# A hybrid decoder layer on one core: row sums of w_ada in PSUM, left factors and weight sums made by VectorE, later keys, other banks

## The chip, the cores and the metric

The kernel runs on one core of one Trainium2 chip. A core has five engines that run their own instruction queues and wait for each other by semaphores: TensorE (PE, matrix products, whose results go to PSUM), VectorE (DVE), ScalarE (ACT), GpSimd (POOL) and SyncE (SP, which here issues every large transfer). [...] The metric is the device time of one execution in microseconds; lower is better.

## The reference

One layer for a sequence of 1024 tokens and a model width of 2048, all in fp32:

```python
mod = silu(c) @ w_ada + b_ada                  # c: (1, 2048), w_ada: (2048, 6144)
shift, scale, gate = split(mod, 3)
h = rms_norm(x, norm_gain) * (1 + scale) + shift
q_sb, k_sb, v_sb, z_sb, q_r, k_r, v_r, z_r = split(h @ w_in)     # w_in: (2048, 8192), 8 parts of 1024
oa = stick_breaking_attention(rms_norm(q_sb), rms_norm(k_sb), v_sb) * silu(z_sb)   # 8 heads of 128
ob = group_norm(chunkwise_retention(rotary(q_r), rotary(k_r), v_r)) * silu(z_r)    # 8 heads of 128
x = x + gate * (concat(oa, ob) @ w_out)        # w_out: (2048, 2048)
```

Stick-breaking attention: `A[t,s] = beta[t,s] * prod_{s<j<t} (1 - beta[t,j])` for s < t, with beta the sigmoid of the scaled scores. Retention: chunks of 128 tokens with a decaying state between them.

## The kernel before

**The products with w_in and w_out** are made with Strassen's scheme on 2 x 2 blocks: seven products P1 to P7 for each pair of 128-column blocks of the weights (a *group*), and sums of blocks on both sides. Each operand is split into a high part in float32r and a low part (the rest), and a product is made of three matmuls of 128 x 128 by 512 columns (high x high, high x low, low x high; `mm3`, L150 to L152). A group's product is a *step* of four such triples. After each triple the program calls `tick()`.

There are 80 groups: *a* (16, tile names e: the first half of the contraction, for attention's columns), *b* (32, names f and g: the second half for attention's columns, then for retention's), *c* (16, names h: the first half for retention's columns), *y* and *o* (8 each: w_out with attention's and with retention's output). All groups of one letter share the *left factor*: seven combinations (A11, S2, S3, A12, S1, A22, S4) of four quarters each, high and low, kept in SBUF. At the change from one letter to the next each combination is replaced, after its last use and before its next one. `place` makes a quarter: ScalarE writes the high part (L146), the low part (L147) is a subtraction, by VectorE for quarters 0 to 2 and by GpSimd for quarter 3. The new values come from SBUF (`gather`, groups b) or are loaded by `take` (groups c, y, o): its `first` loads the four quarters of A11, each when `room(5)` finds five free buffers, and each placed quarter frees its buffer and loads the next combination's.

**The right factors** are the weights. `load` (L246) brings two pieces of 512 KB per group; `make` (L254) makes four sums in place (T1 to T4), on GpSimd; `first` (L259, ScalarE) and `second` (L264, VectorE) make the high and the low part for a product, two steps ahead, into three buffers each. Results leave PSUM by a ScalarE copy (L286) or a VectorE add (L292, L294).

**The order** of all five engines' instructions is written out by the program: `plan` attaches the loads, sums, high and low parts to ticks of the steps (`on`), `run` goes through the steps, and at each tick other work comes in: functions due (`at`), one left quarter every two ticks (`places`), and one step of a task in each of two lanes (a generator that yields how many ticks it waits). If the left factor of the next product is not yet placed (`pending`), `run` calls further ticks without a product until it is. Each engine then works its own queue in order.

**The side work**, with the lines that the text names:

- `second_half`, in groups a: the rows of w_ada for the second half of shift and scale (blocks 0 to 3) and for the gate (blocks 4 to 7), 16 rows of 128 x 512 for each block, one every 2 or 3 ticks, loaded three ahead into four buffers (L605, L608). In blocks 0 to 3 VectorE multiplies each row by its factor and adds it to a sum in SBUF (`weigh`, L434 and L436). In blocks 4 to 7 only the even rows go this way; ScalarE scales the odd ones (L633, L635) and GpSimd adds them to a second sum (L637). At the end of a block TensorE sums over the partitions (`over_partitions`, L414), for one sum or both.
- `keep_left` (L663): GpSimd adds high and low part of each quarter of the left factor and stores it for groups c.
- `sb_heads`: attention, 12 `scores` per head, one every SB_GAP = 7 ticks, and the transposes (`turn`) and value products (`values`, L964) of earlier ones; the next head's keys and queries are split by `split_qk` (L883, L886) at steps 3 and 11. Every step needs three free buffers. When the last head has ended, two more buffers become free, and `ret_heads` follows.
- `ret_heads`: retention, from the time when its columns are ready. Its PSUM tiles share four banks, A0, A1, B and C. `normal` scales the output eight and ten ticks after the last product, `finish` transposes it (L1164) and multiplies it by z.
- `mix_sums`: GpSimd's four combinations of a finished pair of heads (L730 to L740), stored as left factor for groups y and o.

Of the kernel before, what the change touches and what calls it, by code (L numbers as in the profile page):

```python
# [17 lines left out]
P = 128  # L18
# [41 lines left out]
def layer_kernel(ctx, tc, x, c, w_ada, b_ada, norm_gain, w_in, sb_q_gain, sb_k_gain, ret_norm_gain, w_out,  # L60
# [173 lines left out]
    class Group:  # L234
# [11 lines left out]
            nc.sync.dma_start(r, self.w[:, self.k0 + i:self.k0 + 2 * NP:2, self.col0:self.col0 + 2 * P])  # L246
            self.t[f"B{i + 1}1"], self.t[f"B{i + 1}2"] = r[:, :, 0:P], r[:, :, P:2 * P]

        def make(self, n):

            t = self.t
            o, a, op, b = {"T3": ("B12", "B22", ALU.subtract, "B12"), "T2": ("B11", "B12", ALU.add, "B11"),
                           "T1": ("B12", "B22", ALU.subtract, "B11"), "T4": ("B21", "B21", ALU.subtract, "B11")}[n]
            nc.gpsimd.tensor_tensor(t[o], t[a], t[b], op=op)  # L254

        def first(self, p):

# [44 lines left out]
    def on(k, j, fn):  # L302
        events.setdefault((max(k, -9), j), []).append(fn)

    def plan(groups):
        for i, g in enumerate(groups):
            g.n = i
            flat.append((g, "P1"))
            if i:
                flat.extend((groups[i - 1], p) for p in ("P4", "P3"))  # L310
            flat.extend((g, p) for p in ("P6", "P7", "P2", "P5"))
        flat.extend((groups[-1], p) for p in ("P4", "P3"))
        for k, (g, p) in enumerate(flat):
            g.at[p] = k
        for k, (g, p) in enumerate(flat):
            if p == "P1":
                on(k - 7, 0, lambda g=g: g.load(0))
                on(k - 6, 1, lambda g=g: g.load(1))
                on(k - 3, 1, lambda g=g: g.make("T3"))
                alone = g.at["P6"] == k + 1  # L320
                on(k - 2 if alone else k - 1, 3 if alone else 1, lambda g=g: g.make("T2"))
                on(g.at["P5"] - 3, 0, lambda g=g: g.make("T1"))
                on(max(g.at["P4"] - 4, g.at["P2"] - 1), 1, lambda g=g: g.make("T4"))
            if p in OLD:
                on(k - 1, OLD[p][2], lambda g=g, p=p: g.seed is not None and old(g, *OLD[p][:2]))
            on(k - 2, 0, lambda g=g, p=p: g.first(p))
            on(k - 2, 2, lambda g=g, p=p: g.second(p))
# [215 lines left out]
                for i, kd in enumerate(kinds_c)]  # L543
    groups_y = [Group(w_out_k, 0, 256 * i, f"y{i}", put=to_dram(ypart, 2 * i)) for i in range(8)]
    groups_o = [Group(w_out_k, 8, 256 * i, f"o{i}", seed=ypart[2 * i:2 * i + 2]) for i in range(8)]
    plan(groups_a + groups_b + groups_c + groups_y + groups_o)

    def until(g, p):

# [44 lines left out]
    def second_half():  # L594

        order_ = [(i, r) for i in range(8) for r in range(16)]
        src, accs_ = {}, {}

        def load(n):
            if n < len(order_):  # L600
                i, r = order_[n]
                src[i, r] = t = k1b.tile([P, HALF], F32, tag="sg", bufs=4, name=f"ada_b{i}_{r}")
                if i < 4:
                    j = NP + i
                    nc.sync.dma_start(t.rearrange("p (a n) -> p a n", a=2),  # L605
                                      ada_rows[:, r, 0:2, 256 * j:256 * j + 256])
                else:
                    nc.sync.dma_start(t, ada_rows[:, r, 2, HALF * (i - 4):HALF * (i - 3)])  # L608

        def close(i):  # L610
            mod = ps.tile([P, 4], F32, tag="C", name=f"mod_b{i}")
            over_partitions(mod, accs_.pop(i))

            def take_mod():
                if i < 4:
                    ada_mod(NP + i, mod)
                else:
                    k4 = slice(4 * (i - 4), 4 * (i - 3))
                    nc.vector.tensor_tensor(gate_c[:, k4], mod, gate_b[:, k4], op=ALU.add)
            at(3, take_mod)  # L620

        for n in range(3):
            load(n)
        yield 9
        for n, (i, r) in enumerate(order_):
            if r == 0:
                accs_[i] = [k1b.tile([P, HALF], F32, tag="acc", bufs=2, name=f"acc_b{i}")]
            t = src.pop((i, r))
            if i < 4 or r % 2 == 0:
                weigh(accs_[i][0], t, r, r == 0)  # L630
            elif r == 1:
                accs_[i].append(k1b.tile([P, HALF], F32, tag="acc2", bufs=2, name=f"acc2_b{i}"))
                nc.scalar.activation(accs_[i][1], t, AF.Copy, scale=silu_c[:, r:r + 1])  # L633
            else:
                nc.scalar.activation(t, t, AF.Copy, scale=silu_c[:, r:r + 1])  # L635
                a2 = accs_[i][1]
                at(2, lambda a2=a2, t=t: nc.gpsimd.tensor_tensor(a2, a2, t, op=ALU.add))  # L637
            if r == 15:
                at(10, lambda i=i: close(i))
            load(n + 3)  # L640
            yield 2 + n % 2
        yield 16
        for j in range(NP):
            kc = KC // 2 + 2 * j
            a11, a12, a21, a22 = xT[kc, 0], xT[kc + 1, 0], xT[kc, 1], xT[kc + 1, 1]
            for t, k in ((a11, kc), (a21, kc), (a22, kc + 1), (a12, kc + 1)):
                to_h(t, k)
                yield 2
            s1 = k1b.tile([P, HALF], F32, tag="sg", bufs=4, name=f"S1_{j}")
# [21 lines left out]
    def gather(n):  # L671
# [4 lines left out]
            return  # L676
        for j in range(NP):
            def do(j=j):
                place(n, j, staged[n, j], nc.gpsimd if j == 3 else nc.vector)
                if n == "A11":  # L680
                    s2 = staged["S2", j] = staged["A11", j]
                    nc.gpsimd.tensor_tensor(s2, staged["S1", j], s2, op=ALU.subtract)
# [293 lines left out]
    def sb_heads():  # L976
        vts = {}
        for n in range(NS * NH + TURN + 2):
# [21 lines left out]
            if h < NH:  # L1000
# [6 lines left out]
                if nxt < NH and {f"n{nxt}", f"q{nxt}", f"k{nxt}", f"v{nxt}", f"z{nxt}"} <= ready:  # L1007
# [11 lines left out]
                    elif s == 11 and nxt in early:  # L1019
                        yield 2  # L1020
                        split_qk("k", nxt, 0, 0)
                        split_qk("q", nxt, 1, 2)
                        yield SB_GAP - 2
                        continue
            if s == 3 and h < NH:
                yield 3
# [1 line left out]
                turn_v(vts.pop((h, 0)), sbv[h], 0, "A1")  # L1028
                yield 3
                turn_v(vts.pop((h, 1)), sbv[h], 1, "C")  # L1030
                yield SB_GAP - 6
            else:
                yield SB_GAP
        ready.add("sb")
# [22 lines left out]
    def ret_heads():  # L1057
# [4 lines left out]
        for h in range(NH):  # L1062
# [21 lines left out]

            def turn_k(g):
                kds[g] = kd = ht("be", f"kd{g}")
                tp = ps.tile([P, HALF], F32, tag=("C", "A1")[g], name=f"ktp_{h}_{g}")
                for j in range(4):
                    nc.tensor.transpose(tp[:, j * P:(j + 1) * P], k[g][:, j * P:(j + 1) * P], ident)
                at(1, lambda: nc.scalar.activation(kd, tp.rearrange("p (j n) -> p j n", n=P), AF.Copy,  # L1090
# [17 lines left out]
                at(1, update)  # L1108

            def scores_r(g):  # L1110
                sp = ps.tile([P, 4, P], F32, tag=("B", "A1")[g], name=f"sp_{h}_{g}")
                for j in range(4):
                    tk = slice(j * P, (j + 1) * P)
                    nc.tensor.matmul(sp[:, j, :], k[g][:, tk], q[g][:, tk], start=True, stop=True)
# [5 lines left out]
            def values_r(g):  # L1120
# [31 lines left out]
                at(1, stats)  # L1152
                if g:
                    for n, fn in ((2, first_guess), (3, better), (4, better), (5, lambda: better(True)),
                                  (8, lambda: normal(0)), (10, lambda: normal(1))):
                        at(n, fn)
                z = operand(5, f"rz_{h}_{g}", F32) if g else ld(f"rz_{h}_{g}")
                nc.sync.dma_start(z, halves(7 * NH + h, g))
                return on, z

            def finish(g, on, z):
                tp = ps.tile([P, HALF], F32, tag=("B", "A0")[g], name=f"otp_{h}_{g}")
                for j in range(4):
                    nc.tensor.transpose(tp[:, j * P:(j + 1) * P], on[:, j, :], ident)  # L1164

# [67 lines left out]
    def take(src, needs=()):  # L1233
# [7 lines left out]
        def tell(n):  # L1241
# [9 lines left out]
            for j in range(NP):  # L1251

                def do(j=j):
                    t = coming.pop((n, j))
                    place(n, j, t, nc.gpsimd if j == 3 else nc.vector)
                    free(t)
                    load(next_of(n), j)
                place_later(n, do, lambda j=j: (n, j) in coming)
# [108 lines left out]
```

## Time and profile before

| | |
|---|---|
| median of 3 runs | 2044.01 us (2043.52 to 2044.23) |
| profiled execution | 2045.0 us, of which the span is 2043.1 us |
| mean granted TensorE clock | 0.982 |
| busy: PE, DVE, ACT, POOL | 95%, 69%, 43%, 36% of the span |
| transfers | 388 MB, mean 190 GB/s |

The span runs from the first to the last instruction. A row of the timeline gives start and duration in us, engine, line, operation, output<-inputs, and in brackets the idle time before it and what ended it. A row of the groups gives the count, then busy us and mean ns, then the idle time ahead of them. A row of the waits gives us in total, times, and the longest. SPq rows are the issue of a transfer.

### The profile page before, as it was taken

How to read it: one execution, taken by the hardware profiler on the slowest of the kernel's cores; microseconds unless marked ns; L12 is line 12 of the kernel's file. 1: busy time of each engine (PE TensorE's matmuls, PEld its weight loads, DVE VectorE, ACT ScalarE, POOL GpSimd, SP SyncE). 2: the span in 40 equal slices, each digit the busy share in tenths (PEclk: the TensorE clock that was granted, in tenths of full speed). 3: DMA queues.
4: the chain of work that ended last, by engine and by line, in shares of the span. 5: the costliest groups of instructions: out<-in, count | busy, mean ns of one | idle time of the engine just before them, and what ended most of it. 6: DMA issues, size and time to landing. Idle time of an engine off the chain costs nothing. (4 is left out here: it accounts for less than half of the span.)

```text
span 2043.1 us, 26981 instructions
## 1 busy us (share of the span) xinstructions
PE 1949.2 (95%) x9089; PEld 1561.3 (76%) x9089; DVE 1414.5 (69%) x2218; ACT 882.9 (43%) x1598; POOL 737.3 (36%) x507
## 2 busy tenths in 40 slices
PE   5879998998999999999999999899999999999998
PEld 4357777875777777788888888677888887887887
DVE  6668877647557676676666655778787886458655
ACT  4443244454344544545444454544343444345221
POOL 0434478665222223122322322545343444144221
PEclk9879999998999999999999999999999998999999
DMA  9737876633454455443434533867677787457665
GB/s 295 241 114 250 265 261 231 206 98 114 151 189 144 131 171 171 145 139 119 162 104 132 167 107 108 272 212 263 223 245 247 256 290 243 144 165 253 200 203 168
DMA packets 287326, 388.42 MB, mean 190 GB/s; under 512 B 32106, under 2 KB 164276, under 8 KB 287188
## 3 DMA queue, kind: packets, MB, share of 16 engines
q1 hardware_dynamic: 286784, 386.65, 58.5%
q8 instruction: 72, 1.18, 0.2%
q14 instruction: 66, 0.54, 0.1%
q10 hardware_dynamic: 404, 0.05, 0.0%
HBM read 278.51 MB, written 108.10 MB: 189 GB/s over the span
## 5 line engine op out<-in xcount | busy, mean ns | idle before, releaser
L254 POOL TENSOR_TENSOR wr_e<-wr_e,wr_e 128x512 f32<-128x512 f32 x240 | 351.0, 1476 | 746.4 <-DVE wl_e_P L264 679.2
L264 DVE TENSOR_TENSOR wl_e_P<-wr_e,wh_e_P 128x512 fp32r<-128x512 f32 x560 | 494.7, 884 | 119.4 <-ACT wh_e_P L259 119.2
L259 ACT ACTIVATE wh_e_P<-wr_e 128x512 fp32r<-128x512 f32 x560 | 352.0, 630 | 461.7 <-PE b_o L151 56.6
L254 POOL TENSOR_TENSOR wr_e<-wr_e 128x512 f32<-128x512 f32 x80 | 109.4, 1367 | 256.1 <-DVE wl_e_P L264 236.5
L917 DVE TENSOR_TENSOR_SCAN om<-om 128x128 f32<-128x128 f32 (+2 forms) x96 | 111.6, 1163 | 43.7 <-ACT om L908 41.4
L436 DVE SCALAR_TENSOR_TENSOR acc_b<-ada_b,silu_c,acc_b 128x512 f32<-128x512 f32 x88 | 97.9, 1113 | 31.4 <-DMA ada_b<-in_w_ada_dram 30.8
L292 DVE TENSOR_TENSOR pt<-b_f,pt 128x512 f32<-128x512 f32 x64 | 43.9, 687 | 69.3 <-PE b_f L152 69.2
L152 PE MATMUL b_e<-S_h,wl_e_P 128*128 128x512 f32 x192 | 78.7, 410 | 8.9 <-DVE wl_e_P L264 8.7
L150 PE MATMUL b_e<-S_h,wh_e_P 128*128 128x512 f32 x192 | 78.1, 407 | 5.7 <-ACT pt L286 5.7
L908 ACT ACTIVATE om<-zp,rq 128x128 f32<-128x128 f32 (+2 forms) x96 | 56.0, 584 | 61.6 <-PE zp L903 54.0
L151 PE MATMUL b_h<-S_l,wh_e_P 128*128 128x512 f32 x192 | 75.3, 392 | 3.4 <-DVE S_l L147 1.8
L151 PE MATMUL b_e<-S_l,wh_e_P 128*128 128x512 f32 x192 | 77.4, 403 | 0.0
L150 PE MATMUL b_h<-S_h,wh_e_P 128*128 128x512 f32 x192 | 76.7, 400 | 0.5 <-ACT S_h L146 0.5
L964 PE MATMUL oT<-a,v 128*128 128x256 f32 x320 | 76.8, 379 | 0.0
L150 PE MATMUL b_f<-S_h,wh_e_P 128*128 128x512 f32 x192 | 76.5, 399 | 0.0
L152 PE MATMUL b_h<-S_h,wl_e_P 128*128 128x512 f32 x192 | 75.4, 393 | 0.8 <-DVE wl_e_P L264 0.7
L150 PE MATMUL b_g<-S_h,wh_e_P 128*128 128x512 f32 x192 | 75.8, 395 | 0.0
L923 DVE TENSOR_TENSOR be<-be,om 128x127 f32<-128x127 f32 (+2 forms) x96 | 69.9, 728 | 8.0 <-DVE om L917 0.5
L151 PE MATMUL b_f<-S_l,wh_e_P 128*128 128x512 f32 x192 | 75.2, 392 | 0.0
L152 PE MATMUL b_g<-S_h,wl_e_P 128*128 128x512 f32 x192 | 74.9, 390 | 0.0
L152 PE MATMUL b_f<-S_h,wl_e_P 128*128 128x512 f32 x192 | 74.9, 390 | 0.0
L151 PE MATMUL b_g<-S_l,wh_e_P 128*128 128x512 f32 x192 | 74.9, 390 | 0.0
(401 smaller groups left out, 5325.2 us busy)
## 6 DMA issues: line engine op xcount, KB each, us to landing
wr_e<-in_w_in_dram SPq DMA_DIRECT2D x128, 512.0 KB
ada_b<-in_w_ada_dram SPq DMA_DIRECT2D x128, 256.0 KB
part<-pt SPq DMA_DIRECT2D x128, 256.0 KB
pt<-part SPq DMA_DIRECT2D x128, 256.0 KB
fin<-pt SPq DMA_DIRECT2D x128, 256.0 KB
ada_a<-in_w_ada_dram SPq DMA_DIRECT2D x64, 256.0 KB
wr_e<-in_w_out_dram SPq DMA_DIRECT2D x32, 512.0 KB
ld<-fin SPq DMA_DIRECT2D x54, 256.0 KB
```

The lines of the kernel that those rows point to most:

```text
L150: nc.tensor.matmul(o, a_hi, b_hi, start=first, stop=False, skip_group_check=True)
L151: nc.tensor.matmul(o, a_hi, b_lo, start=False, stop=False, skip_group_check=True)
L152: nc.tensor.matmul(o, a_lo, b_hi, start=False, stop=last, skip_group_check=True)
L254: nc.gpsimd.tensor_tensor(t[o], t[a], t[b], op=op)
L259: nc.scalar.activation(hi, self.t[RIGHT[p]], AF.Copy)
L264: nc.vector.tensor_tensor(lo, self.t[RIGHT[p]], self.parts[p].bitcast(F32), op=ALU.subtract)
L292: nc.vector.tensor_tensor(t, src, t, op=ALU.add)
L436: nc.vector.scalar_tensor_tensor(acc, src, cj, acc, op0=ALU.mult, op1=ALU.add)
L908: nc.scalar.activation(om[:, :n], zp[:, :n], AF.Sigmoid, scale=rq[:, h, 1, i:i + 1])
L917: nc.vector.tensor_tensor_scan(rev, rev, rev, init, op0=ALU.mult, op1=ALU.bypass)
L923: nc.vector.tensor_tensor(be[:, :m], be[:, :m], om[:, 1:m + 1], op=ALU.mult)
L964: nc.tensor.matmul(ob, v[:, j, :], a[:, cl], start=diag and ib == 0 and b == 0 and j2 == 0, stop=ch == 0 and ib == 2, skip_group_check=True)
```

## The change

Four edits:

1. In `second_half` a block's sum is now a PSUM tile (banks A0 and A1 in turn), and all 16 rows of each block go through `weigh` on VectorE. Two ticks after the last row ScalarE copies the sum to SBUF, and `over_partitions` takes that one sum.
2. In a set of steps called `crowded`, the 14 from P1 of the last group of a, b, c and y on, `make` is issued on VectorE in place of GpSimd; and `place` makes all four quarters' low parts on VectorE.
3. In `sb_heads` the steps 3 and (where the next head is prepared early) 11 last nine ticks and not seven.
4. In `ret_heads` four kinds of PSUM tiles get other banks, and `normal` runs seven and nine ticks after the last product.

```diff
-        def make(self, n):
+        def make(self, n, eng):
...
-            nc.gpsimd.tensor_tensor(t[o], t[a], t[b], op=op)
+            eng.tensor_tensor(t[o], t[a], t[b], op=op)
...
-    def plan(groups):
+    def plan(groups, lasts):
+
+        crowded = set()
+        def sum_of(g, n, k, j):
+            on(k, j, lambda: g.make(n, nc.vector if k in crowded else nc.gpsimd))
+
...
+        for g in lasts:
+            crowded |= set(range(g.at["P1"], g.at["P3"] + 5))
...
-                on(k - 3, 1, lambda g=g: g.make("T3"))
+                sum_of(g, "T3", k - 3, 1)
                 alone = g.at["P6"] == k + 1
-                on(k - 2 if alone else k - 1, 3 if alone else 1, lambda g=g: g.make("T2"))
-                on(g.at["P5"] - 3, 0, lambda g=g: g.make("T1"))
-                on(max(g.at["P4"] - 4, g.at["P2"] - 1), 1, lambda g=g: g.make("T4"))
+                sum_of(g, "T2", k - 2 if alone else k - 1, 3 if alone else 1)
+                sum_of(g, "T1", g.at["P5"] - 3, 0)
+                sum_of(g, "T4", max(g.at["P4"] - 4, g.at["P2"] - 1), 1)
...
-    plan(groups_a + groups_b + groups_c + groups_y + groups_o)
+    plan(groups_a + groups_b + groups_c + groups_y + groups_o, [gs[-1] for gs in (groups_a, groups_b, groups_c, groups_y)])
...
-        def close(i):
+        def close(i, acc):
             mod = ps.tile([P, 4], F32, tag="C", name=f"mod_b{i}")
-            over_partitions(mod, accs_.pop(i))
+            over_partitions(mod, [acc])
...
             if r == 0:
-                accs_[i] = [k1b.tile([P, HALF], F32, tag="acc", bufs=2, name=f"acc_b{i}")]
-            t = src.pop((i, r))
-            if i < 4 or r % 2 == 0:
-                weigh(accs_[i][0], t, r, r == 0)
-            elif r == 1:
-                accs_[i].append(k1b.tile([P, HALF], F32, tag="acc2", bufs=2, name=f"acc2_b{i}"))
-                nc.scalar.activation(accs_[i][1], t, AF.Copy, scale=silu_c[:, r:r + 1])
-            else:
-                nc.scalar.activation(t, t, AF.Copy, scale=silu_c[:, r:r + 1])
-                a2 = accs_[i][1]
-                at(2, lambda a2=a2, t=t: nc.gpsimd.tensor_tensor(a2, a2, t, op=ALU.add))
+                acc = ps.tile([P, HALF], F32, tag=f"A{i % 2}", name=f"acc_b{i}")
+            weigh(acc, src.pop((i, r)), r, r == 0)
             if r == 15:
-                at(10, lambda i=i: close(i))
+                total = k1b.tile([P, HALF], F32, tag="acc", bufs=2, name=f"acc_s{i}")
+                at(2, lambda total=total, acc=acc: nc.scalar.activation(total, acc, AF.Copy))
+                at(10, lambda i=i, total=total: close(i, total))
...
-                place(n, j, staged[n, j], nc.gpsimd if j == 3 else nc.vector)
+                place(n, j, staged[n, j])
...
                         split_qk("k", nxt, 0, 0)
                         split_qk("q", nxt, 1, 2)
-                        yield SB_GAP - 2
+                        yield SB_GAP
...
                 turn_v(vts.pop((h, 1)), sbv[h], 1, "C")
-                yield SB_GAP - 6
+                yield SB_GAP - 4
...
-                tp = ps.tile([P, HALF], F32, tag=("C", "A1")[g], name=f"ktp_{h}_{g}")
+                tp = ps.tile([P, HALF], F32, tag=("C", "B")[g], name=f"ktp_{h}_{g}")
...
-                sp = ps.tile([P, 4, P], F32, tag=("B", "A1")[g], name=f"sp_{h}_{g}")
+                sp = ps.tile([P, 4, P], F32, tag=("A1", "B")[g], name=f"sp_{h}_{g}")
...
-                                  (8, lambda: normal(0)), (10, lambda: normal(1))):
+                                  (7, lambda: normal(0)), (9, lambda: normal(1))):
...
-                tp = ps.tile([P, HALF], F32, tag=("B", "A0")[g], name=f"otp_{h}_{g}")
+                tp = ps.tile([P, HALF], F32, tag=("A0", "A1")[g], name=f"otp_{h}_{g}")
...
-                    place(n, j, t, nc.gpsimd if j == 3 else nc.vector)
+                    place(n, j, t)
```

More of the change, by code (lines that the diff above doesn't have):

```diff
@@ L596, in second_half @@
         order_ = [(i, r) for i in range(8) for r in range(16)]
-        src, accs_ = {}, {}
+        src = {}
         def load(n):
```

## The prediction

> **What bounds the kernel now.** I read the head of the page, then busy time by stage, then single rows of the stages in which TensorE is not full, then the waits.
>
> ```profile
> span 2043.1 us, 26981 instructions
> PE 1949.2 (95%) x9089; PEld 1561.3 (76%) x9089; DVE 1414.5 (69%) x2218; ACT 882.9 (43%) x1598; POOL 737.3 (36%) x507
> ```
>
> TensorE is busy for 95% of the span, so only what it loses in places can be won. How fast it goes undisturbed is seen in two rows nine matmuls apart: 2.04 us, 0.2267 us each. A tick (three matmuls) is 0.68 us, a group (28 ticks) 19.0 us.
>
> ```profile
> 1297.11 0.39 PE L150 MATMUL b_h<-A_h,wh_e_P 128*128 128x512 f32 x1
> ...
> 1299.15 0.39 PE L150 MATMUL b_h<-A_h,wh_e_P 128*128 128x512 f32 x1
> ```
>
> The stages, with TensorE's busy time and count first, then PEld, DVE, ACT, POOL, and the clock, DMA share and GB/s last:
>
> ```profile
> 150.00:275.00 125.00, 119.58 (x530) 95.87 (x529) 107.06 (x130) 40.62 (x70) 63.10 (x42) 1.00 0.80 257
> 275.00:345.00 70.00, 62.45 (x274) 48.92 (x273) 49.86 (x49) 27.64 (x49) 52.72 (x34) 0.98 0.72 242
> 345.00:445.00 100.00, 99.44 (x444) 81.90 (x443) 61.43 (x62) 50.20 (x84) 65.80 (x44) 0.98 0.55 181
> 445.00:500.00 55.00, 45.90 (x174) 33.10 (x173) 45.12 (x46) 26.06 (x49) 35.71 (x23) 0.91 0.32 105
> ...
> 1295.00:1345.00 50.00, 43.30 (x179) 32.38 (x178) 41.84 (x48) 22.66 (x39) 27.62 (x19) 1.00 0.77 262
> ...
> 1670.00:1710.00 40.00, 35.61 (x158) 28.04 (x157) 34.15 (x67) 22.68 (x46) 18.05 (x13) 0.87 0.69 229
> ...
> 1850.00:1895.00 45.00, 41.99 (x178) 34.11 (x177) 37.43 (x45) 24.39 (x43) 23.69 (x17) 0.96 0.79 260
> ```
>
> The first three rows are w_ada's stage. Of 1248 matmuls 96 are the small ones of L414, 0.116 us each by the row quoted under part 1; 1152 x 0.2267 + 96 x 0.116 = 272.3 of 295 us, so 22.7 us are lost. The other four are the changes of left factor, called seams here, from groups a to b, b to c, c to y and y to o. By the same count they lose 55 - 39.4 = 15.6, 50 - 40.6 = 9.4 and 45 - 40.4 = 4.6 us; the third holds other shapes, so I take idle time plus lost clock: 4.4 + 0.13 x 40 = 9.6 us. Some 62 us are there to be won in all.
>
> Why they are lost shows in single rows:
>
> ```profile
> 153.33 1.77 DVE L436 SCALAR_TENSOR_TENSOR acc_b<-ada_b,silu_c,acc_b 128x512 f32<-128x512 f32 x1
> 155.03 0.68 DVE L264 TENSOR_TENSOR wl_e_P<-wr_e,wh_e_P 128x512 fp32r<-128x512 f32 x1
> 155.63 0.74 DVE L436 SCALAR_TENSOR_TENSOR acc_b<-ada_b,silu_c,acc_b 128x512 f32<-128x512 f32 x1
> 156.30 0.68 DVE L292 TENSOR_TENSOR pt<-a_e,pt 128x512 f32<-128x512 f32 x1
> ```
>
> ```profile
> 152.83 1.73 POOL L663 TENSOR_TENSOR kp_A<-A_h,A_l 128x512 f32<-128x512 f32 x1
> 155.85 1.68 POOL L254 TENSOR_TENSOR wr_e<-wr_e 128x512 f32<-128x512 f32 x1 [1.30 <-DVE wl_e_P L264]
> 159.07 1.29 POOL L663 TENSOR_TENSOR kp_A<-S_h,S_l 128x512 f32<-128x512 f32 x1 [1.53 <-DMA keep_A<-kp_A]
> ```
>
> A VectorE operation with two tensors in SBUF takes 0.68 or 0.74 us (0.60 and 0.67 us from start to start), but up to 1.77 us while GpSimd works; GpSimd's own goes from 1.29 to 1.7 us. The two hold each other up. An operation with one tensor in PSUM doesn't suffer, as its mean over the whole run shows:
>
> ```profile
> L436 DVE SCALAR_TENSOR_TENSOR acc_b<-ada_b,silu_c,acc_b 128x512 f32<-128x512 f32 x88 | 97.9, 1113 | 31.4 <-DMA ada_b<-in_w_ada_dram 30.8
> L292 DVE TENSOR_TENSOR pt<-b_f,pt 128x512 f32<-128x512 f32 x64 | 43.9, 687 | 69.3 <-PE b_f L152 69.2
> L294 DVE SCALAR_TENSOR_TENSOR ot<-b_o,gate_c,ot 128x512 f32<-128x512 f32 x28 | 21.0, 751 | 36.7 <-PE b_o L152 36.7
> ```
>
> **Part 1: w_ada's row sums in PSUM.** For each group of 28 ticks there are 11.2 rows, 7 low parts (L264), 3 adds from PSUM, and on GpSimd 4 weight sums and 2.5 keeps. The work that excludes the other engine is now, in the first four column blocks, 7 x 0.60 + 11.2 x 0.67 + 6.5 x 1.29 = 20.1 us of 19.0; in the gate's blocks, with half the rows on ScalarE and GpSimd, 8.0 + 11.4 x 1.29 = 22.7 us. That is the loss. Afterwards it is 4.2 + 8.4 = 12.6 us, and VectorE's whole work, with 0.75 us for a row in PSUM (L294, the nearest row: one PSUM input, one scalar), is 6.0 + 8.4 = 14.4 us, with some 1.7 us blocked by GpSimd: it fits into 19.0.
>
> No row shows VectorE writing PSUM. The bounds are 0.68 us (L292) and 1.113 us (L436 as it is now). [...]
>
> What stays is w_ada's lateness, now in VectorE's queue alone:
>
> ```profile
> SPq L608 <- POOL acc_b L637: 51.3, 19, 6.6
> ...
> DVE acc_b L436 <- DMA ada_b<-in_w_ada_dram: 30.8, 18, 3.6
> ...
> ACT ada_b L635 <- DMA ada_b<-in_w_ada_dram: 51.0, 22, 5.7
> ```
>
> The 51.3 us in which the load queue waited for GpSimd's release of a buffer go away, and much of ScalarE's 51.0 us with them. But a late row now holds the low parts behind it; these are issued six ticks (4.1 us) ahead of their use, and the longest wait was 3.6 us. ScalarE's new copy out of PSUM, two ticks behind the last row, can hold the high parts queued on ScalarE, eight times. I leave 7 us of the 22.7 (bounds 2 and 15): **gain 15.6**, 8 to 21.
>
> ```profile
> 288.65 1.86 PE L414 MATMUL mod_b<-ones,acc_b 128*128 128x1 f32 x16
> ```
>
> With one sum per block instead of two, each of the gate's four blocks loses 8 of these 16: 32 x 0.116 = **3.7 us** of TensorE's own time.
>
> **Part 2: VectorE at the seams.** In each, 7 low parts and 8 weight sums move from GpSimd to VectorE.
>
> ```profile
> 454.43 3.77 POOL L254 TENSOR_TENSOR wr_e<-wr_e,wr_e 128x512 f32<-128x512 f32 x3
> ...
> 455.75 0.63 ACT L259 ACTIVATE wh_e_P<-wr_e 128x512 fp32r<-128x512 f32 x1 [3.93 <-POOL wr_e L254]
> ...
> 456.99 1.75 DVE L147 TENSOR_TENSOR S_l<-xT,S_h 128x512 fp32r<-128x512 f32 x1 [5.05 <-POOL wr_e L254]
> ```
>
> Here VectorE stands still for 5.05 us while GpSimd works off its queue. Seam a-b: 46 operations took 45.12 us, which at 0.62 are 28.5; so 23 of GpSimd's cost VectorE 16.6, 0.7 each. Afterwards 61 x 0.62 + 8 x 0.7 = 43.4 us against TensorE's 39.4: VectorE sets the pace by a little, I leave 6 of 15.6 us: **gain 9.6** (4 to 12). Seam c-y: 34.15 - 13 x 0.63 + 12 x 0.62 = 33.4 us against 30.4; **gain 4.6** (0 to 8). Seam y-o: 37.43 - 17 x 0.63 + 13 x 0.62 = 34.8 against 40.4; **gain 3** (0 to 4.6). The sums on VectorE wait for the weights' load where GpSimd did; the low parts would be queued behind.
>
> **Part 3: two ticks more for keys.** What they can win is one wait, above all:
>
> ```profile
> 766.82 0.39 PE L902 MATMUL zp<-k,q 128*128 128x256 f32 x1 [2.41 <-DVE k L886]
> ```
>
> With smaller ones I count **3 us** (0 to 3.7). But a head now takes 88 ticks and not 84: eight times 2 at step 3 and seven times 2 at step 11, 30 in all, of which three waits for room absorb some 2 each. So attention ends 24 ticks later, and at seam b-c something waits for that end:
>
> ```profile
> 1261.06 1.39 SPq L716 DMA_DIRECT2D ld<-keep_A  x3
> ...
> 1287.11 0.32 SPq L397 DMA_DIRECT2D mix_A<-ld  x1
> ...
> 1287.96 0.44 SPq L716 DMA_DIRECT2D ld<-keep_A  x1
> ```
>
> ```profile
> 1292.36 0.62 ACT L146 ACTIVATE A_h<-ld 128x512 fp32r<-128x512 f32 x1
> ```
>
> ```profile
> 1284.47 1.89 PE L964 MATMUL oT<-a,v 128*128 128x256 f32 x8
> ```
>
> Three of A11's four parts are loaded 27 us ahead; the fourth needs five free buffers, and gets them only when the last head's output is stored and its buffers are freed. From the last L964 to the first b_h product at 1297.11 lie 16 ticks, from the head's end, seven ticks on, 9. Take 24 off: P1 of groups c is written out with some 15 ticks ahead of it that hold only the rest of attention. On TensorE: L964, then three quarters of P1 (2.0 us), while output, store and load take from 1286.4 to 1287.96, the landing until 1292.36, the parts another 1.3: 7.3 us, a stall of 5.3. All placements follow in this order, so the chain that was issued 9.1 us ahead of P1 starts 1.7 us behind: up to 10.8 us more loss, which VectorE's relief lessens (DMA at 0.77 there). The four loads, four stores and four GpSimd sums of the last head pair come as much later, and are needed only at seam c-y. **Loss 8** (from 16 lost to 4 won). [...]
>
> **Part 4: retention's banks.**
>
> ```profile
> PE otp L1164 <- ACT v L757: 1.5, 3, 0.7
> ```
>
> The first output transposes leave the bank B, which the next head's values hold until four ticks before. Their new bank, A0, held the output itself, so its release is the copy that they need anyway; the second ones' A1 is read out six ticks before. The two normalisations come one tick earlier. The other banks dealt anew show no wait now, and none is freed later than a step before its use: nothing. **Gain 1.5** (0 to 3).
>
> **Sum.** 15.6 + 3.7 + 9.6 + 4.6 + 3 + 3 - 8 + 1.5 = 33.0 us off the profiled execution, 2045.0 (span 2043.1 and 1.9 around it): 2012. The runs' median, 2044.0, is 1.0 lower: **2011 us**. The worst ends of all terms add to about nothing, the best to 60 us.
>
> **Rivals.** *The later end of attention costs nothing* (2000): if heads wait less for room than I count, or a buffer comes free earlier, b-c gains 3 instead of losing 8. For it: 9 ticks of slack now; against: 24 is well above 9. *VectorE becomes the bound at the seams* (2033): no seam gains, w_ada's stage gains 12: 12 + 3.7 - 8 + 3 = 10.7 us. For it: 43.4 against 39.4 us in the first seam; against: the standstill of 5.05 us belongs to GpSimd's queue. *PSUM rows are slow, slower than before* (2067): VectorE reads and writes the same bank in each row. From (19.0 - 6.0 - 1.7) / 11.2 = 1.0 us a row VectorE sets the pace of 320 ticks; at 1.3 us it has eaten all gains ((22.7 + 17.4) / 11.4 = 3.5 us a group); at 1.5 us a group takes 24.5 us, 11.4 groups 63 us more, less 22.7 now lost, less the 17.4 of the other parts: 23 us slower. For it: no row shows the write; against: L294 and L292 at one length under GpSimd's load. *The rows come no sooner* (2026): if bandwidth and not release makes them late (share 0.80, 257 GB/s), that stage gains nothing: 33.0 - 15.6.
>
> **Chances.** Forecast 0.50 (own range 2002 to 2021); attention free 0.14; VectorE the bound 0.16; rows no sooner 0.10; slow PSUM 0.10. The range 1996 to 2037 leaves out slow PSUM and the tails. A measurement tells 0.2% (4 us): faster 0.87, same 0.04 (the worst ends, and rows in PSUM near 1.3 us), slower 0.09.
>
> **What would show it.** Right: L436's successor at 0.68 to 0.80 us, no GpSimd adds, w_ada's stage down to some 276 us of 295; the wait of 5.05 us in seam a-b gone; the fourth load of keep_A late and a TensorE stall of 4 to 8 us ahead of the first b_h; no wait on L886. Wrong: rows above 1.0 us, seams as long as before, or that load ahead of P1.

## The result, and the profile after

The changed kernel takes 2012.4 us (median of 4 runs, 2011.2 to 2016.5) against 2043.8 us before; the ratio is 0.9855, with a 95% interval of 0.9839 to 0.9871. The forecast was 2011 us. The profiled execution took 2011.25 us with a span of 2009.4 us. What follows shows that the sum came out right although three of its terms did not: that their errors nearly cancelled was luck.

The head of the page of the changed kernel, and from its groups the row sums of w_ada (what was L436 is now L443; count, then busy us and mean ns, then the idle time ahead):

```profile
span 2009.4 us, 26906 instructions
PE 1930.7 (96%) x9057; PEld 1555.4 (77%) x9057; DVE 1372.0 (68%) x2310; ACT 867.1 (43%) x1574; POOL 584.9 (29%) x419
L443 DVE SCALAR_TENSOR_TENSOR acc_b<-ada_b,silu_c,acc_b 128x512 f32<-128x512 f32 x120 | 90.0, 750 | 16.7 <-DMA ada_b<-in_w_ada_dram 15.4
```

A row with its sum in PSUM takes 0.750 us, as L294 did; in SBUF it took 1.113 us on average. GpSimd's busy time went from 737 to 585 us. VectorE has 92 instructions more and is busy for 42 us less.

Stages of the changed kernel, with the columns of the prediction's table (length; busy time and count of PE, PEld, DVE, ACT, POOL; clock, DMA share, GB/s):

```profile
150.00:275.00 125.00, 125.00 (x569) 104.12 (x568) 103.40 (x149) 43.17 (x75) 56.92 (x42) 1.00 0.88 286
275.00:345.00 70.00, 70.00 (x323) 58.42 (x322) 54.68 (x79) 23.61 (x42) 30.80 (x23) 1.00 0.90 298
417.00:425.00 8.00, 8.00 (x36) 6.36 (x35) 8.00 (x8) 4.30 (x9) 5.09 (x4) 1.00 0.29 100
425.00:440.00 15.00, 12.70 (x54) 9.62 (x53) 15.00 (x20) 8.33 (x16) 6.35 (x4) 1.00 0.25 79
440.00:457.00 17.00, 13.78 (x58) 11.11 (x58) 17.00 (x29) 9.80 (x19) 0.00 (x0) 0.94 0.31 101
...
1258.00:1268.00 10.00, 7.28 (x25) 5.28 (x24) 4.58 (x9) 3.86 (x7) 0.00 (x0) 0.83 0.74 240
1268.00:1300.00 32.00, 26.42 (x96) 18.13 (x94) 26.71 (x38) 15.49 (x27) 6.15 (x4) 0.95 0.88 299
```

In the first two rows TensorE is never idle: the loss of w_ada's stage is gone, and the rows come faster (0.88 and 0.90 of the transfer engines instead of 0.80 and 0.72), so bandwidth didn't hold them. In the next three, seam a-b, VectorE is busy without a gap for 40 us and GpSimd stands still at the end. The last two are seam b-c, where clock and TensorE fall.

To compare stages between kernels I take the time from tick to tick. A tick's first triple begins with a weight load of L150; so w_ada's stage, ticks 84 to 432, runs in the kernel before from 183.03 to 453.51 us, 270.5 us:

```profile
183.03 0.19 PEld L150 LDWEIGHTS b_e<-S_h,wh_e_P 128*128 128x128 f32 x1
...
453.51 0.19 PEld L150 LDWEIGHTS a_e<-A_h,wh_e_P 128*128 128x128 f32 x1
```

and in the changed one from 180.84 to 423.78 us, 242.9 us:

```profile
180.84 0.19 PEld L150 LDWEIGHTS b_e<-S_h,wh_e_P 128*128 128x128 f32 x1
...
423.78 0.19 PEld L150 LDWEIGHTS a_e<-A_h,wh_e_P 128*128 128x128 f32 x1
```

All stages and all kernels below in this way, in us (seam b-c is contained in the column before it, seam c-y in the column before it; the last column is the median of the runs):

| kernel | w_ada 84-432 | a-b 432-500 | 672-1400 | b-c 1328-1400 | 1400-2032 | c-y 1776-1820 | y-o 2032-2044 | time |
|---|---|---|---|---|---|---|---|---|
| before | 270.5 | 66.8 | 686.0 | 58.9 | 525.2 | 45.5 | 13.2 | 2043.8 |
| changed | 242.9 | 61.8 | 690.6 | 68.8 | 525.0 | 45.1 | 9.8 | 2012.4 |
| e1, part 1 alone | 242.9 | 66.0 | 686.6 | 59.5 | 526.7 | 45.8 | 14.3 | 2016.6 |
| e2, without part 3 | 242.9 | 60.8 | 686.7 | 59.6 | 525.0 | 45.1 | 12.3 | 2007.4 |
| e3, without part 2 | 242.9 | 66.8 | 692.0 | 70.1 | 525.4 | 45.8 | 14.1 | 2024.1 |
| e4, early fourth load | 242.9 | 60.6 | 675.5 | 53.7 | 525.5 | 45.0 | 12.0 | 1998.9 |
| e5, e4 without part 3 | 242.9 | 60.5 | 680.1 | 53.0 | 526.3 | 45.1 | 9.8 | 1999.8 |
| e6, e4, quarters GpSimd | 242.9 | 60.4 | 675.1 | 53.2 | 527.2 | 46.7 | 14.1 | 2001.4 |
| e7, e4, sums GpSimd | 242.9 | 63.3 | 676.3 | 54.4 | 524.1 | 45.4 | 9.9 | 1998.1 |
| e8, e4 without part 4 | 242.9 | 60.5 | 675.9 | 54.1 | 526.9 | 45.4 | 9.9 | 1998.3 |
| e9, before, early load | 270.0 | 65.1 | 681.7 | 53.0 | 526.0 | 45.4 | 13.4 | 2036.3 |
| e10, no low parts in seams | 242.9 | 53.2 | 675.6 | 53.7 | 523.6 | 42.2 | 9.8 | 1985.2 |
| e11, sums in SBUF | 261.8 | 60.8 | 675.5 | 53.6 | 525.6 | 45.7 | 9.8 | 2013.7 |
| e12, e4, sums VectorE in a-b only | 242.9 | 60.5 | 676.6 | 54.8 | 525.5 | 46.1 | 10.0 | 1995.2 |

In e5 one run of four, at 3923.8 us, is left out, and the median is that of the other three; e10 has one run. The columns of stages come from one trace of each kernel. Most stages that a kernel leaves untouched come out within some tenths, but the start up to tick 84 scatters (179.0 to 183.3 us), ticks 1400 to 2032 by about 1 us, and the seams by up to 2.5: a-b takes 65.1 to 66.8 us in the four kernels that have it as before (before, e1, e3, e9), y-o 9.8 to 12.3 where it is as in the changed kernel. So the change divides up as: w_ada 27.6 us won, a-b 5.0 won, attention with seam b-c 4.6 lost, c-y and retention 0.2 won (within the scatter), y-o 3.4 won (1 to 4.5 by that scatter), the start 2.2 (scatter): 33.8, the difference of the spans being 33.7. The medians differ by 31.4.

Seam b-c of the changed kernel, its load queue, then ScalarE and TensorE:

```profile
1218.58 1.40 SPq L716 DMA_DIRECT2D ld<-keep_A  x3
...
1259.77 0.32 SPq L404 DMA_DIRECT2D mix_A<-ld  x1
1260.14 0.42 SPq L716 DMA_DIRECT2D ld<-keep_A  x1
```

```profile
1263.12 0.63 ACT L146 ACTIVATE A_h<-ld 128x512 fp32r<-128x512 f32 x1 [8.06 <-DMA ld<-keep_A]
```

```profile
1257.12 1.89 PE L964 MATMUL oT<-a,v 128*128 128x256 f32 x8
1258.66 0.58 PE L150 MATMUL b_h<-A_h,wh_e_P 128*128 128x512 f32 x1
...
1263.80 0.79 PE L150 MATMUL b_h<-A_h,wh_e_P 128*128 128x512 f32 x1 [2.72 <-ACT A_h L146]
```

The last L964 is now directly ahead of the first b_h product, and the fourth load of keep_A is issued 1.5 us behind that product, right after the last head's output is stored. P1 runs through three quarters and waits 2.72 us for the fourth.

### The profile page after: what moved, and what is told of

The parts are those of the page before. It is cut to its first block, busy times and chain, and to the rows that moved or that the text cites. A ratio compares the mean times of both kernels' runs of the same rounds, so it can differ in the third digit from the quotient of the medians.

```text
span 2009.4 us, 26906 instructions
## 1 busy us (share of the span) xinstructions
PE 1930.7 (96%) x9057; PEld 1555.4 (77%) x9057; DVE 1372.0 (68%) x2310; ACT 867.1 (43%) x1574; POOL 584.9 (29%) x419
## 3 DMA queue, kind: packets, MB, share of 16 engines
q1 hardware_dynamic: 286784, 386.65, 59.5%
## 5 line engine op out<-in xcount | busy, mean ns | idle before, releaser
L254 POOL TENSOR_TENSOR wr_e<-wr_e,wr_e 128x512 f32<-128x512 f32 x216 | 302.9, 1416 | 881.8 <-DVE wl_e_P L264 708.1
L264 DVE TENSOR_TENSOR wl_e_P<-wr_e,wh_e_P 128x512 fp32r<-128x512 f32 x560 | 451.8, 807 | 131.2 <-ACT wh_e_P L259 129.8
L254 POOL TENSOR_TENSOR wr_e<-wr_e 128x512 f32<-128x512 f32 x72 | 94.2, 1308 | 231.4 <-DVE wl_e_P L264 214.5
L917 DVE TENSOR_TENSOR_SCAN om<-om 128x128 f32<-128x128 f32 (+2 forms) x96 | 106.8, 1113 | 64.7 <-ACT om L908 62.7
L443 DVE SCALAR_TENSOR_TENSOR acc_b<-ada_b,silu_c,acc_b 128x512 f32<-128x512 f32 x120 | 90.0, 750 | 16.7 <-DMA ada_b<-in_w_ada_dram 15.4
L150 PE MATMUL b_e<-S_h,wh_e_P 128*128 128x512 f32 x192 | 75.8, 395 | 5.7 <-ACT pt L286 5.7
L150 PE MATMUL b_h<-S_h,wh_e_P 128*128 128x512 f32 x192 | 77.9, 406 | 1.2 <-ACT S_h L146 1.2
L964 PE MATMUL oT<-a,v 128*128 128x256 f32 x320 | 76.8, 379 | 0.0
L150 PE MATMUL b_f<-S_h,wh_e_P 128*128 128x512 f32 x192 | 76.6, 399 | 0.0
L150 PE MATMUL b_g<-S_h,wh_e_P 128*128 128x512 f32 x192 | 75.6, 394 | 0.0
L286 ACT ACTIVATE pt<-b_e 128x512 f32<-128x512 f32 x48 | 28.8, 599 | 98.2 <-PE b_e L152 92.8
```

What stands on the lines that cost most here:

```text
L150: nc.tensor.matmul(o, a_hi, b_hi, start=first, stop=False, skip_group_check=True)
L254: eng.tensor_tensor(t[o], t[a], t[b], op=op)
L264: nc.vector.tensor_tensor(lo, self.t[RIGHT[p]], self.parts[p].bitcast(F32), op=ALU.subtract)
L286: nc.scalar.activation(t, src, AF.Copy, scale=1.0 if gt is None else gt)
L443: nc.vector.scalar_tensor_tensor(acc, src, cj, acc, op0=ALU.mult, op1=ALU.add)
L917: nc.vector.tensor_tensor_scan(rev, rev, rev, init, op0=ALU.mult, op1=ALU.bypass)
```

## The experiments

**e1: part 1 alone.** Into the kernel before, only the new `second_half`:

```diff
-                accs_[i] = [k1b.tile([P, HALF], F32, tag="acc", bufs=2, name=f"acc_b{i}")]
+                acc = ps.tile([P, HALF], F32, tag=f"A{i % 2}", name=f"acc_b{i}")
...
+            weigh(acc, src.pop((i, r)), r, r == 0)
```

> The kernel before with part 1 alone: w_ada's rows summed in PSUM by VectorE, everything else as before. In the trace of the changed kernel w_ada's stage (ticks 84 to 432) takes 27.6 us less. Theory A, part 1 does this by itself (the sums leave the SBUF that VectorE and GpSimd exclude each other from): 2043.8 - 27.6 = 2016, between 2013 and 2019. Theory B, part 1 gives what the prediction booked (15.6 + 3.7 = 19.3) and the other 8 us come from the rest of the change: 2024 to 2025. L443's mean 0.75 us in both.

Measured: 2016.6 us (ratio to before 0.9859, 0.9834 to 0.9885); ticks 84 to 432 take 242.9 us, exactly as with the whole change. Theory A: the stage's 27.6 us belong to part 1, and the other three parts together are worth only some 4 us more.

**e11: the same rows on VectorE, but the sums in SBUF** (on top of e4, below, which doesn't touch this stage):

```diff
-                acc = ps.tile([P, HALF], F32, tag=f"A{i % 2}", name=f"acc_b{i}")
+                acc = k1b.tile([P, HALF], F32, tag="acc", bufs=2, name=f"acc_b{i}")
...
-                at(2, lambda total=total, acc=acc: nc.scalar.activation(total, acc, AF.Copy))
```

> The run with the early fourth load, but w_ada's sums lie in SBUF again, all 16 rows of each block still summed by VectorE (no scaled rows of ScalarE, no adds of GpSimd, no copy out of PSUM). Theory A, VectorE and GpSimd excluding each other in SBUF is the loss: 20.1 us of such work per group of 19.0 us, rows at about 1.1 us each, ticks 84 to 432 take 8 to 16 us more than 242.9, 2007 to 2015. Theory B, the loss was the gate's odd rows on their way through ScalarE and GpSimd, which held the load buffers: rows at 0.75 to 0.85 us, ticks 84 to 432 within 3 us of 242.9, 1999 to 2002.

Measured: 261.8 us for ticks 84 to 432 and 2013.7 us in all, 18.9 us more for the stage. The group of the rows, and the first of the stages:

```profile
L443 DVE SCALAR_TENSOR_TENSOR acc_b<-ada_b,silu_c,acc_b 128x512 f32<-128x512 f32 x120 | 122.9, 1024 | 24.5 <-DMA ada_b<-in_w_ada_dram 23.5
150.00:275.00 125.00, 119.04 (x527) 95.00 (x526) 107.58 (x137) 37.39 (x64) 55.62 (x37) 1.00 0.80 259
```

The same instruction takes 1.024 us with its sum in SBUF and 0.750 with it in PSUM, and the DMA share falls back to 0.80. Theory A, if a little above its 8 to 16. That GpSimd is the cause, and not the place of the sum by itself, is seen row by row: of the 120 rows of this group in e11's trace, the 54 that no GpSimd operation overlaps take 0.745 us on average and the 66 others 1.252; in the changed kernel it is 0.749 and 0.750. The first four blocks end near tick 172. In ticks 84 to 172 e11 takes 70.7 us, the kernel before 70.0 and the changed one 61.6: there the rows held up by GpSimd are the whole loss. In ticks 252 to 432, in the gate's later blocks, e11 takes 130.4 where before took 139.1, while in ticks 84 to 252 both take 131.4. So 8.7 us came from the gate's odd rows; 2.8 are the halved L414 of the last three blocks (24 x 0.116), and the other 5.9, by subtraction, the rows' way through ScalarE and GpSimd. So 18.9 + 8.7 = 27.6.

**e2: part 3 undone.**

```diff
-                        yield SB_GAP
+                        yield SB_GAP - 2
...
-                yield SB_GAP - 4
+                yield SB_GAP - 6
```

> The changed kernel with part 3 undone: steps 3 and 11 of a head last seven ticks again. Theory A, attention's later end makes the seam b-c 9.8 us longer and the nine ticks win about 5.3 us within attention: the seam is 59 us again instead of 68.7, the wait on L886's k comes back, and the time is 2012.4 - 9.8 + 5.3 = 2008, between 2005 and 2010. Theory B, the seam b-c is longer because weight sums and fourth quarters moved to VectorE there: the seam stays at 66 us or more, and the time is 2012.4 + 5.3 - 0 to 2 = 2016 to 2018.

Measured: 2007.4 us (2003.9 to 2009.9), seam b-c 59.6 us. Theory A; weight sums and quarters on VectorE do not lengthen this seam. Part 3 made the kernel slower by 5.0 us (3.9 by ticks 672 to 1400).

**e4: the fourth load early, nine ticks kept.**

```diff
-            yield from room(3)
+            yield from room(3 if n < NS * (NH - 1) + 4 else 1)
...
-                        yield from room(5)
+                        yield from room(4 if j == NP - 1 else 5)
```

> The changed kernel with one thing more: the fourth load of A11 for groups c needs four free buffers and not five, and the last head's steps from the fifth on need one free buffer and not three, so that this load is issued right behind the third. Theory A, P1 of groups c is late because this load waits for the end of attention: the load lies 20 us or more ahead of P1, the stall of TensorE ahead of the first b_h goes, the seam b-c takes 58 to 61 us instead of 68.7, and the time is 2002 to 2005. Theory B, the seam is bound by the loads and stores of its whole chain (DMA share 0.77) or by VectorE, and only the first wait goes: 2008 to 2012.

Measured: 1998.9 us (1998.1 to 2001.8; ratio to before 0.9774, 0.9754 to 0.9794), better than theory A. The load queue, and the seam as a window, with that of the changed kernel behind it:

```profile
1217.28 1.88 SPq L716 DMA_DIRECT2D ld<-keep_A  x4
...
1250.00:1304.00 54.00, 52.59 (x229) 41.90 (x228) 45.10 (x65) 25.30 (x44) 11.29 (x8) 1.00 0.82 274
```

```profile
1251.00:1320.00 69.00, 59.88 (x228) 44.62 (x227) 45.59 (x67) 27.84 (x47) 11.27 (x8) 0.93 0.69 227
```

The same 228 or 229 matmuls in 54 us instead of 69, at full clock, with the same work on VectorE. That the whole chain behind the fourth load had been late is seen in ScalarE's waits of the changed kernel (here a late one, 1.51 us), and in the transfers, which fill their engines there (shares of 1.03 and 1.01, as the profile counts them):

```profile
1293.15 0.63 ACT L146 ACTIVATE A_h<-a 128x512 fp32r<-128x512 f32 x1 [1.51 <-DMA a<-keep_A]
...
1268.00:1273.00 5.00, 5.00 (x24) 4.11 (x23) 4.31 (x7) 2.63 (x5) 0.00 (x0) 1.00 1.03 347
1273.00:1278.00 5.00, 4.00 (x18) 2.99 (x16) 4.28 (x3) 3.10 (x6) 4.76 (x4) 1.00 1.01 361
```

**e9: only that, in the kernel before.** Same edit, on top of the kernel before.

> The kernel before with only the early fourth load (four free buffers needed instead of five; the last head's later steps need one and not three). Theory A, the fourth load waited for the end of attention in the kernel before too, so the nine ticks that the prediction took as free were not: seam b-c 53 to 55 us instead of 58.9, 2044 - 5 = 2039. Theory B, as the prediction has it, that load was in time with seven ticks and the seam lost its 9.4 us to GpSimd and VectorE: 58 to 60 us, 2043 to 2045.

Measured: seam b-c 53.0 instead of 58.9 us, 2036.3 us (ratio to before 0.9963, 0.9947 to 0.9978). Theory A: with seven ticks the load was in time for P1, but not for the chain behind it. By ticks 672 to 1400 the gain is 4.3 us, by the ratio some 7.6.

**e5: e4 with seven ticks**, e2's edit on top of e4.

> The run with the early fourth load, and part 3 undone beside it (seven ticks at steps 3 and 11). Theory A, the two changes answer for different things: the seam b-c stays at 53 to 55 us and attention takes 5.3 us more (7.6 lost between ticks 672 and 1232, 2.3 won between 1232 and 1328), so 1998.9 + 5.3 = 2004, between 2003 and 2006. Theory B, with attention ending 24 ticks sooner the seam wins more than that (under 50 us), and seven ticks are at least as good: 1999 or less.

Measured: 1999.8 us (1999.7 to 2003.4), between the two theories. Ticks 672 to 1400 take 680.1 us against 675.5, and the seam 53.0: theory A in kind, with too high a price. The 5.3 us that I had read off ticks 672 to 1328 contained work that only moved behind them (4.6 up to tick 1400), and in the two traces 3.2 us of it are masked by the scatter of start and seam y-o (1.0 and 2.2 us longer in e4's). By the waits, nine ticks are worth 2.6 us (e5, then e4, over the whole span):

```profile
PE zp L902 <- DVE k L886: 3.7, 6, 2.4
```

```profile
PE zp L902 <- DVE k L886: 1.1, 1, 1.1
```

So part 3 wins some 1 (by the medians) to 4.6 us (by the ticks) where the load doesn't wait for attention's end, and loses 4 to 5 where it does.

**e3: part 2 undone.**

```diff
-            on(k, j, lambda: g.make(n, nc.vector if k in crowded else nc.gpsimd))
+            on(k, j, lambda: g.make(n, nc.gpsimd))
...
-                    place(n, j, t)
+                    place(n, j, t, nc.gpsimd if j == 3 else nc.vector)
```

> The changed kernel with part 2 undone: weight sums and the fourth quarters' low parts on GpSimd again. Theory A, VectorE's relief of GpSimd is worth what the traces differ by: 5.0 at a-b, 0.4 at c-y, 3.4 at y-o, so 2012.4 + 8.8 = 2021, between 2018 and 2024. Theory B, GpSimd's own operations were slow at the seams mostly because VectorE worked in SBUF beside them, and w_ada's sums are out of the way now: 2010 to 2015, no difference. The wait of some 5 us on L254 in seam a-b comes back under A.

Measured: 2024.1 us, so part 2 is worth 11.7 us; by ticks 5.0 at a-b, 1.4 up to tick 1400, 0.4 behind it, 4.3 at y-o. Theory A, at its upper end. The wait of 5 us in seam a-b is back, as long as before (the changed kernel has none):

```profile
DVE S_l L147 <- POOL wr_e L254: 5.1, 1, 5.1
```

**e6 and e7: half of part 2 undone each, on top of e4.** e6 has the fourth quarters' low parts on GpSimd, e7 the weight sums (the two lines of e3's diff, one in each).

> The run with the early fourth load, with the fourth quarters' low parts on GpSimd again and the weight sums left on VectorE. Theory A, an SBUF operation of GpSimd holds VectorE up by about what VectorE saves (0.7 against 0.62 us): the seam a-b stays at 60 to 62 us, the time at 1998 to 2001. Theory B, VectorE alone is the bound at the seams (100% busy from 424 to 458 us, with GpSimd idle for the second half of it) and seven operations fewer shorten each: a-b 56 to 57 us, 1990 to 1995.

> The run with the early fourth load, with the weight sums on GpSimd again and the fourth quarters' low parts left on VectorE. Theory A, the gain of part 2 (some 11 us by the run without it) is the weight sums': on GpSimd they are late, and high and low parts wait for them, a-b 65 to 67 us and 2006 to 2009. Theory B, it is the fourth quarters': 1999 to 2002.

Measured: e6 2001.4 us, with a-b at 60.4 us: theory A there, seven operations less on VectorE and no gain: from tick 432 to 500 VectorE is busy for 45.1 us with 59 operations where e4 has 43.9 with 65. It loses 1.7 us at c-y and 2 to 4 at y-o. e7 1998.1 us: a-b 63.3, but elsewhere nothing lost, and in the median (e4 1998.9) the 2.7 us at a-b don't show. Neither theory of e7 holds as written: the gain at a-b is not one half's or the other's. Undone together they cost 6 us there (66.8 against 60.6), the sums alone 2.7, the quarters alone nothing. At y-o the quarters carry it (14.1 in e6, 9.9 in e7).

**e10: VectorE relieved at two seams**, on top of e4: in the 14 steps of a-b and c-y `second` is left out, and the high part of the weights stands in for the low part.

```diff
-        def second(self, p):
+        def second(self, p, bare=False):
+            if bare:
+                self.parts[p] = self.parts[p], self.parts[p]
+                return
```

> The run with the early fourth load, and in the 14 steps of the seams a-b and c-y no low parts of the weights are made: the high part stands in their place, so TensorE's work is the same and VectorE has 14 operations (8.7 us) less in each (the products are then without the weights' low parts there). Theory A, VectorE is the bound of both seams: a-b from 60.6 to 53 to 55 us, c-y from 45.0 to 40 to 42 us. Theory B, a-b is VectorE's but c-y is held by retention's own chain of small operations: a-b as under A, c-y 44 to 45 us. Theory C, neither: a-b 59 us or more.

Measured, in one run: a-b 53.2 instead of 60.6 us, c-y 42.2 instead of 45.0. Theory A at a-b: VectorE is its bound now. c-y lies between the theories: VectorE has a part of 2.8 us, and the longest wait of the seam stayed. It is the one ahead of retention's output transposes (L1164; L1168 in e10). Here e10, then the changed kernel, each with rows of TensorE and ScalarE:

```profile
1639.62 1.12 PE L1168 MATMUL otp<-ident,be 128*128 128x128 f32 x4 [3.58 <-ACT be L1154]
...
1637.02 0.63 ACT L827 ACTIVATE a<-pt 128x512 f32<-128x512 f32 x1 [3.28 <-DVE pt L295]
```

```profile
1659.90 0.50 PE L152 MATMUL d_y<-S_h,wl_e_P 128*128 128x512 f32 x1 [1.67 <-DVE wl_e_P L264]
1665.50 0.66 PE L1164 MATMUL otp<-ident,be 128*128 128x128 f32 x4 [3.71 <-ACT be L1150]
...
1662.91 0.63 ACT L823 ACTIVATE ld<-pt 128x512 f32<-128x512 f32 x1 [3.83 <-DVE pt L292]
1663.96 1.49 ACT L1150 ACTIVATE be<-op,m,y 128x128 f32<-128x128 f32 x4
```

In the changed kernel retention's scaling (L1150) is queued on ScalarE behind L823, which waits 3.83 us for VectorE's add. In e10 VectorE has less to do, yet the same link stands: ScalarE's L827 (the same line, four further down) waits 3.28 us for the same add (there L295). So the weights' low parts are at most a small part of what makes that add late; which of VectorE's other operations in the queue ahead of it are the rest was not separated.

**e8: part 4 undone, on top of e4** (old banks, `normal` one tick later).

> The run with the early fourth load, with part 4 undone: retention's old banks and normalisations one tick later. Theory A, as predicted, the banks are worth 1.5 us, between ticks 1500 and 2032: 2000.4. Theory B, they are worth nothing: ticks 1400 to 2032 take within 0.7 us of the same, 1998 to 1999.5. Theory C, the second output transposes' bank A1 makes them worth less than nothing: 1997.

Measured: 1998.3 us against 1998.9; ticks 1400 to 2032 526.9 against 525.5, while e5, which has part 4, took 526.3. In ticks 1500 to 2032, where theory A puts the gain, e8 takes 451.3 us and e4 452.2. Theory B as far as this can be told: nothing beyond the scatter.

**e12: weight sums on VectorE at a-b alone**, on top of e4:

```diff
-    plan(groups_a + groups_b + groups_c + groups_y + groups_o, [gs[-1] for gs in (groups_a, groups_b, groups_c, groups_y)])
+    plan(groups_a + groups_b + groups_c + groups_y + groups_o, [groups_a[-1]])
```

> The run with the early fourth load, with weight sums made by VectorE only in the seam a-b (there they were worth 2.7 us) and by GpSimd in the others; the fourth quarters' low parts stay on VectorE. Theory A, the seams add up: a-b 60.6, b-c 54.4, c-y 45.4, ticks 1820 to 2032 0.7 us less: 1998.9 - 0.5, that is 1997 to 1999. Theory B, the 0.7 to 1.3 us less between ticks 1500 and 2032 were scatter: 1999 to 2000.

Measured: 1995.2 us (1993.8 to 1997.3), ratio to before 0.9758 (0.9742 to 0.9774). That is below both theories, and it beats both kernels, the changed one by some 17 us. From e4 it is not told apart: the intervals overlap, the seams b-c and c-y are 1.1 us longer in its trace, and most of its lead in the median isn't found there.

## Why the prediction was right, point by point

**Part 1** was booked at 15.6 + 3.7 = 19.3 us and gave 27.6. The mechanism was right: GpSimd's operations hold VectorE's rows up in SBUF (e11: 1.252 us for a row beside one, 0.745 alone, 18.9 us in all), and the gate's odd rows cost on top (8.7 with L414). The size lies outside the term's own bounds (8 to 21, with the 3.7 at most 24.7). The mis-sized step is "I leave 7 us of the 22.7": nothing is left. VectorE's waits for rows fell to 15.4 us with none over 2.0 (before 30.8, longest 3.6), and none of them reached TensorE, which has no gap in the whole stage:

```profile
DVE acc_b L443 <- DMA ada_b<-in_w_ada_dram: 15.4, 15, 2.0
```

The value of 0.75 us for the row that no trace showed, taken from the nearest one (L294), measured 0.750. With both tensors in SBUF the row took 1.024 us on average (e11), with one in PSUM 0.750, GpSimd being busy for nearly as long (55.6 and 56.9 us from 150 to 275 us). The operand in PSUM itself cost next to nothing: an undisturbed row took 0.745 us in SBUF.

**Part 2**, a-b: 9.6 booked, 5.0 measured, inside its bounds. The step that failed is again the rest left, "I leave 6 of 15.6": VectorE at 43.4 against 39.4 us did not set the pace "by a little", it set it for 40 us without a gap (e10: 7.4 us hang on 14 of its operations). Totals over the seam hid that VectorE's work is bunched there. The standstill of 5.05 us did go. The rival *VectorE becomes the bound at the seams* was right on the place and wrong on the size, since the seam still gained. c-y: 4.6 booked, 0.4 measured. The step took the whole loss for GpSimd's and VectorE's; but VectorE's time in the seam hardly fell, the sums and quarters having moved to it (39.65 us of 45.5 before, 38.65 of 45.0 after):

```profile
1665.50:1711.00 45.50, 41.11 (x185) 32.71 (x185) 39.65 (x72) 25.35 (x49) 23.03 (x16) 0.89 0.70 232
```

```profile
1635.00:1680.00 45.00, 39.08 (x186) 31.14 (x185) 38.65 (x86) 25.40 (x49) 5.03 (x4) 0.96 0.67 224
```

and the largest wait was retention's, which no count of operations shows. y-o: 3 booked, 3.4 measured, with a scatter nearly as large; the quarters did it (e6, e7).

**Part 3**: 3 won and 8 lost were booked, net 5 lost; undoing it brought 5.0. The mechanism, the fourth load that needs the end of attention, is shown by e4. The distribution was off: the seam lost 9.9 us and not 8, ticks 672 to 1328 won 5.1 and not 3 (one wait of 1.1 us on L886 is left). TensorE's stall at P1 was 2.7 us, not 5.3, and under the 4 to 8 us named as a sign. The prediction had taken the load's landing from ScalarE's row at 1292.36, 4.4 us behind the issue; but that row has no wait in brackets, so the load had landed before ScalarE came to it. Where ScalarE does wait (the 8.06 us above), the part follows the issue by 3.0 us. More of the loss came behind the stall, from the chain and the clock: the mean clock of 0.93 over 69 us is 4.8 us. And the seam's own loss, which the prediction saw only as something that VectorE's relief would lessen, was for 5.9 us the same late load (e9): the nine ticks counted as slack were slack for P1 alone. The rival *the later end of attention costs nothing* is refuted (e2).

**Part 4**: 1.5 booked, nothing measurable.

So the sum of 33.0 us held (31.4 by the medians), but by luck: with 8.3 us too little for w_ada against 4.6 too much at a-b, 4.2 at c-y and 1.5 for the banks, and 2.2 us of scatter in the start beside them in the traces. The rivals *PSUM rows are slow* and *the rows come no sooner* fell with 0.750 us a row and with a transfer share of 0.88 to 0.90 where it had been 0.72 to 0.80.

## What to carry to other kernels

Where VectorE and GpSimd hold each other up in SBUF, moving an operation from one to the other may win nothing (e6: a-b 60.4 us against 60.6 in e4), while here putting one operand into PSUM removed the conflict (rows at 0.750 us instead of 1.024 in e11, 18.9 us). When a task is stretched, look for what waits on its end; a load that is in time for its first user can still be late for the chain that follows it, and two lines that let it go earlier were worth 13.5 us, nearly half as much as the whole change. Book no remainder by feeling: the two terms whose "rest" was guessed (7 of 22.7, 6 of 15.6) were off in opposite directions, and one experiment that takes the suspected work or place away (e10, e11) measures the rest.

## What the runs showed of the hardware that was not expected

The clock fell after gaps of 2.72 us and less. In the changed kernel's seam b-c it is halved three times, for 3.41 us each time. Here are the stretches of 3.41 us ahead of each and at half clock (TensorE's busy time first, clock third from the end); the third row is the stretch ahead of the fourth:

```profile
1260.42:1263.83 3.41, 0.69 (x4) 0.23 (x3) 0.05 (x1) 0.71 (x2) 0.00 (x0) 1.00 0.86 277
1263.83:1267.24 3.41, 3.41 (x7) 2.40 (x8) 3.06 (x6) 3.15 (x6) 0.00 (x0) 0.50 0.91 296
1277.48:1280.90 3.42, 1.89 (x6) 0.97 (x6) 3.42 (x5) 1.80 (x4) 1.82 (x2) 1.00 0.75 276
1280.90:1284.31 3.41, 1.73 (x7) 1.08 (x7) 3.41 (x7) 1.26 (x2) 0.00 (x0) 1.00 0.69 188
1284.31:1287.72 3.41, 3.41 (x10) 2.66 (x9) 3.03 (x6) 1.48 (x3) 0.00 (x0) 0.50 0.72 238
1297.97:1301.38 3.41, 1.78 (x5) 0.72 (x5) 1.99 (x3) 1.31 (x3) 0.00 (x0) 1.00 1.06 397
1301.38:1304.79 3.41, 3.41 (x8) 2.55 (x9) 2.20 (x4) 1.62 (x3) 1.28 (x1) 0.50 0.69 258
```

The first drop follows one gap of 2.72 us. Ahead of the second the longest gap is 1.44 us, ahead of the third 0.60:

```profile
1282.40 0.50 PE L151 MATMUL a_h<-A_l,wh_e_P 128*128 128x512 f32 x1 [1.44 <-DVE A_l L147]
...
1298.54 0.49 PE L150 MATMUL b_h<-S_h,wh_e_P 128*128 128x512 f32 x1 [0.58 <-ACT S_h L146]
...
1300.60 0.49 PE L150 MATMUL b_h<-S_h,wh_e_P 128*128 128x512 f32 x1 [0.60 <-ACT S_h L146]
```

What the three have in common is that TensorE was busy for little more than half of the 3.41 us or less (0.69, 1.73 and 1.78 us); after 1.89 us (the third row) the clock stayed at 1.00. With so few cases, and with matmul ends that the profile models, this is a reading and not a measured limit. Still, ahead of the second and the third drop no gap was over 1.44 us: the chain that arrived in pieces was paid for twice here, once in waits and once, with some 5 us (three times 3.41 us at half clock), in the clock.
